# Interleaving two arrays: eight 32 KiB-row tiles in six buffers, or six 43 KiB-row tiles woven in place

## The chip, the cores and the metric

The kernel runs on one core of a Trainium2 chip. The metric is the device time of one execution in microseconds (us), as the median of several runs; lower is better. Five engines take part in different ways: SyncE (SP) and ScalarE (ACT) only issue DMAs here, VectorE (DVE) copies, TensorE and GpSimd do nothing for the result. All DMAs, from whichever queue, are carried by the core's 16 DMA engines, called rings here when one of them is meant.

## The reference

```python
batch, seq, dim = 32, 256, 1024          # x and y: float32, 33.6 MB each
result = np.zeros((batch, seq, dim * 2), dtype=np.float32)
result[..., 0::2] = x
result[..., 1::2] = y
```

Since `dim` is the last axis and contiguous, this is one interleaving of two flat arrays of 8,388,608 words: output word 2i is x[i], output word 2i+1 is y[i]. Nothing is calculated. 67.1 MB are read and 67.1 MB written.

## The kernel before

The flat arrays are cut into n = 8 tiles of 128 partitions with W = 8192 words (32 KiB) a partition. Each tile has 4 MiB of x, 4 MiB of y and 8 MiB of output. Six buffers of 32 KiB a partition are used: two for x (`xt`), two for y (`yt`) and two for woven output (`ot`). A tile's output does not fit into one `ot` buffer, so it is made in two halves h = 0 and 1, each of H = 4096 words of x and of y, and half h always uses `ot[h]`.

Three engines run one program each, tied together by semaphores:

- **SP, the loads.** L42 and L43 load the first x in two halves; these two DMAs are moved to the front of the program, ahead of the opening barrier. Then, for each tile, L50 loads x and L53 loads y. From the third tile on, L48 holds x until VectorE has done the last copy that reads this x buffer, and L52 holds y in the same way. The semaphore is `woven`, which VectorE raises after every copy.
- **VectorE, the weave.** For each half, L67 copies x into the even words of `ot[h]` and L70 copies y into the odd words. L60 and L69 wait for the loads. L64 waits until the earlier store of this `ot[h]` has landed. A landing counts 16 on a DMA's semaphore.
- **ACT, the stores.** L83 issues the store of a half when both its copies are done. The very first half is sent in two pieces, a quarter of its columns (8 KiB a row, L77) and the rest (24 KiB a row, L81).

The end (L87 to L93) waits for the last stores and clears the semaphores. The order of DMAs within a queue is the order of these loops; between the queues the hardware decides.

Of the kernel before, what the change touches and what calls it, by code (L numbers as in the profile page):

```python
# [3 lines left out]


def _interleave(nc, x, y, out):
    P = 128
    W = 8192
    H = W // 2  # L10

    total = 1
    for s in x.shape:
        total *= s
    n = total // (P * W)
    assert n * P * W == total

    def rows(ap, names, k):
        flat = ap.rearrange("b s d -> (b s d)")
        return flat[k * names : (k + 1) * names].rearrange("(p w) -> p w", p=P)  # L20

    fp32 = mybir.dt.float32
    xt = [nc.alloc_sbuf_tensor(f"xt{b}", [P, W], fp32).ap() for b in (0, 1)]
    yt = [nc.alloc_sbuf_tensor(f"yt{b}", [P, W], fp32).ap() for b in (0, 1)]
    ot = [nc.alloc_sbuf_tensor(f"ot{b}", [P, W], fp32).ap() for b in (0, 1)]

    xsem = [nc.alloc_semaphore(f"xsem{b}") for b in (0, 1)]
    hsem = nc.alloc_semaphore("hsem")
    qsem = nc.alloc_semaphore("qsem")
    ysem = [nc.alloc_semaphore(f"ysem{b}") for b in (0, 1)]  # L30
    woven = nc.alloc_semaphore("woven")
    osem = [nc.alloc_semaphore(f"osem{b}") for b in (0, 1)]


    cuts = [0, W // 4, W]
    parts = [slice(a, b) for a, b in zip(cuts, cuts[1:])]

    xs = [rows(x, P * W, k) for k in range(n)]
    ys = [rows(y, P * W, k) for k in range(n)]
    os_ = [rows(out, 2 * P * W, k) for k in range(n)]  # L40

    nc.sync.dma_start(out=xt[0][:, :H], in_=xs[0][:, :H]).then_inc(xsem[0], 16)  # L42
    nc.sync.dma_start(out=xt[0][:, H:], in_=xs[0][:, H:]).then_inc(hsem, 16)  # L43

    for k in range(n):
        b = k % 2
        if k >= 2:
            nc.sync.wait_ge(woven, 4 * (k - 2) + 3)  # L48
        if k:
            nc.sync.dma_start(out=xt[b], in_=xs[k]).then_inc(xsem[b], 16)  # L50
        if k >= 2:
            nc.sync.wait_ge(woven, 4 * (k - 2) + 4)  # L52
        nc.sync.dma_start(out=yt[b], in_=ys[k]).then_inc(ysem[b], 16)  # L53

    for k in range(n):
        b = k % 2
        for h in (0, 1):
            c = slice(h * H, (h + 1) * H)
            if h == 0:
                nc.vector.wait_ge(xsem[b], 16 * (k // 2 + 1))  # L60
            elif k == 0:
                nc.vector.wait_ge(hsem, 16)
            if k:
                nc.vector.wait_ge(osem[h], 16 * k)  # L64
            if (k, h) == (1, 0):
                nc.vector.wait_ge(qsem, 16)
            nc.vector.tensor_copy(out=ot[h][:, 0::2], in_=xt[b][:, c]).then_inc(woven, 1)  # L67
            if h == 0:
                nc.vector.wait_ge(ysem[b], 16 * (k // 2 + 1))  # L69
            nc.vector.tensor_copy(out=ot[h][:, 1::2], in_=yt[b][:, c]).then_inc(woven, 1)  # L70

    for k in range(n):
        for h in (0, 1):
            nc.scalar.wait_ge(woven, 4 * k + 2 * h + 2)
            if (k, h) == (0, 0):
                for c in parts[:-1]:
                    nc.scalar.dma_start(  # L77
                        out=os_[k][:, c], in_=ot[h][:, c]
                    ).then_inc(qsem, 16)
                c = parts[-1]  # L80
                nc.scalar.dma_start(out=os_[k][:, c], in_=ot[h][:, c]).then_inc(osem[h], 16)  # L81
                continue
            nc.scalar.dma_start(  # L83
                out=os_[k][:, h * W : (h + 1) * W], in_=ot[h]
            ).then_inc(osem[h], 16)

    nc.scalar.wait_ge(osem[0], 16 * n)  # L87
    used = sorted(s.num for s in [*xsem, hsem, qsem, *ysem, woven, osem[0]])
    assert used == list(range(used[0], used[-1] + 1)), used
    nc.scalar.sem_clear(range(used[0], used[-1] + 1))  # L90
    nc.sync.nop(nofuse=True).wait_op(osem[1], 16 * n, "sem-ge").then_inc(
        osem[1], -16 * n
    )  # L93


def kernel(tc, x, y, out):
    nc = tc.nc
    tc.close()
    tc.compile()

    _interleave(nc, x, y, out)

    blocks = nc.main_func.blocks
    for engine in (mybir.EngineType.SP, mybir.EngineType.SP):
        opening = blocks[0].instructions
        at, moved = next(
            (b, i)
            for b in blocks[1:]
            for i in b.instructions
            if i.engine == engine and i.opcode == "DMACopy"  # L110
        )
        assert not (moved.sync_info and moved.sync_info.on_wait)
        body = at.instructions
        body.remove(moved)
        gate = next(
            n
            for n, i in enumerate(opening)
            if i.engine == engine and i.opcode == "Drain"
        )
        opening.insert(gate, moved)  # L120
        at.instructions = body
        blocks[0].instructions = opening


# [1 line left out]
_INS = ['x', 'y']  # L126
_OUTS = [((32, 256, 2048), 'float32')]


# [23 lines left out]
```

## Time and profile before

| | |
|---|---|
| median of 3 runs | 314.21 us (314.18 to 314.25) |
| span of the profiled execution, first to last instruction | 312.9 us |
| time of the profiled execution | not listed apart; the median stands 1.35 us above the span of 312.86 |
| VectorE busy | 72.0 us, 32 copies of 2.29 us |
| DMA | 34 DMAs, 4896 packets, 134.22 MB, 429 GB/s over the span |
| HBM | 67.11 MB read, 67.11 MB written |
| store of 4 MiB, from issue to landing | 34.1 us median |
| load of y, 4 MiB, from issue to landing | 41.5 us median |

How to read it: a DMA's time from issue to landing holds the time that it stands in its queue behind others, so 34 us for 4 MiB says nothing of the speed of a transfer. The busy share of the DMA engines does, and the rate in GB/s beside it. In the timeline a row is an instruction (start, duration, engine, line, operation); for a DMA the duration is that of issuing it, not of the transfer. A bracket behind a row tells how long the engine had been idle and what released it.

### The profile page before, as it was taken

Reading aid. Unit: us, or ns where it says so; the run is one execution under the profiler, and the core shown is the slowest. Engines: PE = TensorE matmul, PEld = TensorE weight load, DVE = VectorE, ACT = ScalarE, POOL = GpSimd, SP = SyncE. Lnnn points to the kernel's source line nnn. Section 1 sums busy time; section 2 is a strip of 40 time slices with the busy share of each in tenths; the row PEclk is TensorE's granted clock in tenths of the full one; section 3 lists DMA queues with packets and bytes.
Section 4 is the critical chain, followed back from the end, with each engine's and each line's share of the span. In section 5 each row is a group of like instructions: output and inputs, shape, how many; then the busy total and the mean of one; then the engine's idle time right before and its main releaser. Section 6 shows DMA issues by size and latency. Waiting matters only on the chain.

```text
span 312.9 us, 114 instructions
## 1 busy us (share of the span) xinstructions
DVE 72.0 (23%) x32; POOL 0.2 (0%) x4
## 2 busy tenths in 40 slices
DVE  0216000501305023050220503205032050415410
POOL 0000000000000000000000000000000000000000
DMA  8999999999999999999999999999999999999998
GB/s 337 467 402 436 436 402 419 452 457 415 427 444 411 461 402 469 402 469 402 469 402 465 406 440 432 423 448 402 469 402 469 402 469 402 469 402 448 423 423 381
DMA packets 4896, 134.22 MB, mean 429 GB/s; under 512 B 544, under 2 KB 544, under 8 KB 544
## 3 DMA queue, kind: packets, MB, share of 16 engines
q1 hardware_dynamic: 2448, 67.11, 50.1%
q10 hardware_dynamic: 2448, 67.11, 49.7%
HBM read 67.11 MB, written 67.11 MB: 429 GB/s over the span
## 4 chain that ended last, share of the span: by engine, by line
DMA 82%; DVE 12%; issue 0%
DMA out_dram<-ot 76%; DMA yt<-in_y_dram 6%; DVE ot L70 6%; DVE ot L67 6%
## 5 line engine op out<-in xcount | busy, mean ns | idle before, releaser
L67 DVE COPY ot<-xt 128x4096 f32<-128x4096 f32 x16 | 36.7, 2295 | 213.8 <-DMA out_dram<-ot 206.5
L70 DVE COPY ot<-yt 128x4096 f32<-128x4096 f32 x16 | 36.6, 2288 | 12.3 <-DMA yt<-in_y_dram 12.3
L137 POOL MEMSET const-bfloat16-1.0<- 128x1 bf16 x1 | 0.1, 103 | 0.0
L137 POOL MEMSET const-uint8-127<- 128x1 uint8 x1 | 0.1, 102 | 0.0
L137 POOL MEMSET const-float32-0.0<- 128x1 f32 x1 | 0.1, 100 | 0.2 <-issue 0.2
L137 POOL MEMSET const-float32-1.0<- 128x1 f32 x1 | 0.1, 99 | 0.0
## 6 DMA issues: line engine op xcount, KB each, us to landing
out_dram<-ot ACTq DMA_DIRECT2D x15, 4096.0 KB, 34.1
yt<-in_y_dram SPq DMA_DIRECT2D x8, 4096.0 KB, 41.5
xt<-in_x_dram SPq DMA_DIRECT2D x7, 4096.0 KB, 24.3
xt<-in_x_dram SPq DMA_DIRECT2D x2, 2048.0 KB, 9.5
out_dram<-ot ACTq DMA_DIRECT2D x1, 3072.0 KB, 32.8
out_dram<-ot ACTq DMA_DIRECT2D x1, 1024.0 KB, 16.3
```

Of the source, the lines that this page charges most:

```text
L67: nc.vector.tensor_copy(out=ot[h][:, 0::2], in_=xt[b][:, c]).then_inc(woven, 1)
L70: nc.vector.tensor_copy(out=ot[h][:, 1::2], in_=yt[b][:, c]).then_inc(woven, 1)
L137: nc = _bacc.Bacc("TRN2", target_bir_lowering=False, num_devices=1)
```

## The change

The arrays are cut into six tiles, five with rows of 11008 words (43 KiB) and one with 10496 (41 KiB). Two regions `R[0]` and `R[1]` of 86 KiB a partition take the tiles in turn. A tile's x is loaded into the region's first half and its y into its second half, and the woven output is made in the same region: the low half of the output where x was, the high half where y was.

Weaving in place needs an order in which nothing is overwritten before it is read. VectorE first copies the upper half of x into a third buffer, `park`. It then spreads the lower half of x onto the even words of the low region in pieces that halve each time, from the top down (2752 words, 1376, and so on to 43); the last piece goes through the small buffer `last`, because its source and target overlap. When y is there, one copy puts the lower half of y on the odd words: the low half is complete and can be stored. Then the upper half of y is spread within its own region in the same way, and the parked x is laid on its even words. These are 21 copies a tile, 126 in all, and each waits for the one before it through the semaphore `step`.

The stores are one DMA for each half tile, 12 in all, and the loads 13 (the first x still in two pieces, of 4096 and 6912 words). From the third tile on SP holds the x load until the low half's store from that region has landed (`lsem`), and the y load until the high half's has (`hsem`). The two first loads are moved to the front as before, and the end waits for the last landings as before.

```diff
+TILES = [11008] * 5 + [10496]
+FIRST = 4096
...
-    xt = [nc.alloc_sbuf_tensor(f"xt{b}", [P, W], fp32).ap() for b in (0, 1)]
-    yt = [nc.alloc_sbuf_tensor(f"yt{b}", [P, W], fp32).ap() for b in (0, 1)]
-    ot = [nc.alloc_sbuf_tensor(f"ot{b}", [P, W], fp32).ap() for b in (0, 1)]
+    R = [nc.alloc_sbuf_tensor(f"R{b}", [P, 2 * N_MAX], fp32).ap() for b in (0, 1)]
+    park = nc.alloc_sbuf_tensor("park", [P, N_MAX // 2], fp32).ap()
+    last = nc.alloc_sbuf_tensor("last", [P, 64], fp32).ap()
...
+    def copy(to, of):
+        nonlocal count
+        if count:
+            nc.vector.wait_ge(step, count)
+        nc.vector.tensor_copy(out=to, in_=of).then_inc(step, 1)
+        count += 1
+
+    def halvings(m):
+        while m > 64:
+            assert m % 2 == 0
+            yield m // 2, m
+            m //= 2
+        yield 0, m
+
+    done = []
+    for k, N in enumerate(TILES):
+        b = k % 2
+        h = N // 2
+        X = R[b][:, :N]
+        Y = R[b][:, N : 2 * N]
+        low = R[b][:, :N]
+        high = R[b][:, N : 2 * N]
+
+        if k == 0:
+            nc.vector.wait_ge(fsem, 16)
+        nc.vector.wait_ge(xsem[b], 16 * (k // 2 + 1))
+        copy(park[:, :h], X[:, h:])
+        for i, j in halvings(h):
+            if i:
+                copy(low[:, 2 * i : 2 * j : 2], X[:, i:j])
+            else:
+                copy(last[:, :j], X[:, :j])
+                copy(low[:, 0 : 2 * j : 2], last[:, :j])
+        nc.vector.wait_ge(ysem[b], 16 * (k // 2 + 1))
+        copy(low[:, 1::2], Y[:, :h])
+        done.append([count])
+        for i, j in halvings(h):
+            i, j = h - j, h - i
+            if j < h:
+                copy(high[:, 2 * i + 1 : 2 * j : 2], Y[:, h + i : h + j])
+            else:
+                copy(last[:, : j - i], Y[:, h + i : h + j])
+                copy(high[:, 2 * i + 1 : 2 * j : 2], last[:, : j - i])
+        copy(high[:, 0::2], park[:, :h])
+        done[-1].append(count)
+
+    nc.sync.dma_start(out=R[0][:, :FIRST], in_=xs[0][:, :FIRST]).then_inc(fsem, 16)
+    nc.sync.dma_start(
+        out=R[0][:, FIRST : TILES[0]], in_=xs[0][:, FIRST:]
+    ).then_inc(xsem[0], 16)
+    for k, N in enumerate(TILES):
         b = k % 2
         if k >= 2:
-            nc.sync.wait_ge(woven, 4 * (k - 2) + 3)
+            nc.sync.wait_ge(lsem[b], 16 * (k // 2))
         if k:
-            nc.sync.dma_start(out=xt[b], in_=xs[k]).then_inc(xsem[b], 16)
+            nc.sync.dma_start(out=R[b][:, :N], in_=xs[k]).then_inc(xsem[b], 16)
         if k >= 2:
-            nc.sync.wait_ge(woven, 4 * (k - 2) + 4)
-        nc.sync.dma_start(out=yt[b], in_=ys[k]).then_inc(ysem[b], 16)
+            nc.sync.wait_ge(hsem[b], 16 * (k // 2))
+        nc.sync.dma_start(out=R[b][:, N : 2 * N], in_=ys[k]).then_inc(ysem[b], 16)
...
+    for k, N in enumerate(TILES):
         b = k % 2
...
+        for c, sem, ready in zip((0, N), (lsem[b], hsem[b]), done[k]):
+            nc.scalar.wait_ge(step, ready)
+            nc.scalar.dma_start(
+                out=os_[k][:, c : c + N], in_=R[b][:, c : c + N]
+            ).then_inc(sem, 16)
```

## The prediction

> **What bounds the kernel now.** I began with the page: the busy slices, the packet count and the two queues.
>
> ```profile
> DVE  0216000501305023050220503205032050415410
> ...
> DMA  8999999999999999999999999999999999999998
> ...
> DMA packets 4896, 134.22 MB, mean 429 GB/s; under 512 B 544, under 2 KB 544, under 8 KB 544
> ...
> q1 hardware_dynamic: 2448, 67.11, 50.1%
> q10 hardware_dynamic: 2448, 67.11, 49.7%
> ```
>
> The 16 DMA rings are busy in every slice; VectorE works a quarter of the time. q1 (SP's loads) and q10 (ACT's stores) split the span. 4896 packets are 34 DMAs of 128 rows (4352) and 16 semaphore packets for each (544): one row is one packet, whatever its length. Then the windows, for a stretch without start or end:
>
> ```profile
> 60.00:260.00 200.00, 47.04 (x21) 0.00 (x0) 1.00 1.00 433
> ```
>
> DMA share 1.00 at 433 GB/s. So the large waits are not losses, which is how I read this view:
>
> ```profile
> DVE ot L67 <- DMA out_dram<-ot: 206.5, 14, 29.0
> DVE ot L70 <- DMA yt<-in_y_dram: 12.3, 1, 12.3
> ```
>
> VectorE waits 206.5 us for output buffers while the rings work. Only two things can move the end: what a ring spends beside bytes, and moments in which it has no packet. The timeline shows the beginning and the end:
>
> ```profile
> 0.00 0.37 SPq L42 DMA_DIRECT2D xt<-in_x_dram  x1
> ...
> 21.91 2.29 DVE L70 COPY ot<-yt 128x4096 f32<-128x4096 f32 x1 [12.28 <-DMA yt<-in_y_dram]
> 24.12 2.29 DVE L67 COPY ot<-xt 128x4096 f32<-128x4096 f32 x1
> 24.24 0.38 ACTq L77 DMA_DIRECT2D out_dram<-ot  x1
> ...
> 293.53 2.29 DVE L67 COPY ot<-xt 128x4096 f32<-128x4096 f32 x1 [5.14 <-DMA out_dram<-ot]
> ```
>
> Stores land at 293.5 and, with the span's end, at 312.9: two stores in 19.3 us, 9.67 each, the full rate to the last row. Copies start 2.21 us apart for 4096 elements: 0.54 ns an element.
>
> The rest comes from the trace's packet records. On one ring, rows of 8, 16 and 32 KiB follow each other after 305.6, 606.6 and 1209.4 ns: bytes at 27.2 GB/s plus 4.2 ns a packet. A semaphore packet adds 6 ns. With both queues filled, a ring takes one row from each in turn. A ring carries 8.389 MB: 308.4 us, plus 272 rows x 4.2 ns = 1.14 and 34 x 6 ns = 0.20. The first row starts at 0.99 and the first rows are slow, 2.1 us in all. The sum is 311.85; the last packet ends at 312.48 and its count lands at 312.83. The missing 0.6 us stands in the load rows beside the first stores (27 to 43 us), which take up to 1.55 us in place of 1.21: 0.55 us a ring.
>
> The span is 312.86. The execution's own time is not listed apart; the runs' median, 314.21, is 1.35 above the span, and I keep these 1.35.
>
> **The change, part by part.** *Fewer, longer rows.* The DMAs fall from 34 to 25 (13 loads, 12 stores), the rows of a ring from 272 to 200. That is 72 x 4.2 ns = 0.30 us and 9 x 6 ns = 0.05 us, together **-0.36 us**, all on the path. A 43 KiB row at this law takes 1.623 us. No row over 32 KiB is in the trace; the law held over a factor of four, so I use it. The bounds: at best the whole overhead goes (-1.3); if each long row became two packets there would be 384 rows, 112 more than now, +0.5.
>
> *The first store.* Its 8 KiB piece (L77) goes; the first store now has 43 KiB rows. The 0.55 us of slow load rows lies just there: about 0.2 in the row before the first store row appears, 0.25 beside the 8 KiB rows, 0.07 at the second store. If it belongs to the beginning of writing it stays, if to short rows half of it goes. Bounds 0 and -0.55; I take **-0.15**, nearer to staying, because the largest part precedes the short rows.
>
> *When the first store starts.* x0 and y0 are 8 x 606.6 + 8 x 1020.7 + 8 x 1623 ns = 26.0 us, after the 2.1: y0's last row ends at 28.1 and not at 21.5. It costs nothing: x1 and y1 are queued (26 us of rows). Landing 0.38 after the last row, odd copy 5504 x 0.54 = 3.0, issue at 31.6. In the trace the first store row came 4.40 us after its issue (24.24 to 28.64), so 36.0 here; meanwhile four or five load rows run alone. From there rows alternate.
>
> *Loads that wait for stores.* L48 and L52 waited for the copy that had read a buffer; now the x of tile k+2 waits until the low store of tile k has landed, its y for the high one. Behind that wait on SP stands only the next y; VectorE would wait for both. Low 0 (8 pairs of 3.25 us) ends at 62, while x1 and y1 feed the rings until 72: some 9 us ahead, and as both queues then advance row for row this lead stays to tile 5. The Trainium skill's page "DMA: Bandwidth & Descriptors" (Anatomy of one DMA) speaks against this edit: most of a fixed 2 us lies between last byte and semaphore, worst with HBM as target. The trace has 0.35 us there, at a store (312.48 to 312.83); by the page 1.65 us more would come off a lead of 9, and the same off the tail's margin below.
>
> *The weave.* 126 copies for 32, 21 a tile, each waiting for the one before on `step`. Elements: four halves of 5504 a tile, 11.9 us. The 18 short ones add a fixed cost, not shown for DVE here; between 0.08 us (2.29 busy against 2.21 apart) and 0.3 us, three of the 0.10 us memsets. So 13 to 17 us a tile, up to 100 in all, under 52 us of DMA a tile. Parking x and spreading its half is done while y is still in transfer, a 26 us cover. Only the odd copy of the low half stands between y and a store: low 1 can be issued at 75.5 and is due when high 0 ends, at 88. If this cover were gone, every microsecond late would count once.
>
> *The tail*, where I expected a loss. When y5's last row ends, at E, the loads are over. After y0 there are 80 load rows a ring and as many store rows of tiles 0 to 4; they pair one for one, so the stores behind are as many as the load rows that ran alone before the first store: four or five, 6.5 to 8.1 us. E is near 278. Low 5 is issued at E + 0.38 + 2.85 + 0.05 = E + 3.3, so the rings stay fed if its first row comes within 3.2 us. The trace has two latencies: 0.99 us (first load, nothing else queued) and 4.40 us (first store, two whole loads queued on SP). In the tail SP is empty and ACT's rows go on, so I take the first: no gap, **0**, with 2 us or more to spare. High 5 is issued by E + 12, due at E + 19. The last two stores are 16 x 1.548 us.
>
> The Trainium skill has a rule that would change the tail: the same page (Queues, rings and completion order) lets a ring drain a packet of some 9 to 17 descriptors from one queue before it turns to the other. Nine are a whole DMA's share here; high 4 would then be untouched at E, 13 us of cover. The trace alternates single rows, so I keep 6.5.
>
> Sum: 314.21 - 0.36 - 0.15 = **313.7**.
>
> **The rivals.** *Faster, 313.2 to 313.5:* the slow load rows vanish with the 8 KiB piece: -0.36 - 0.55 = 313.3. For it: the second and third slow rows alternate with 8 KiB rows, and no later store shows any. Against it: the first slow row comes before any store row.
>
> *Slower, 314.9 to 315.4:* a gap in the tail. If low 5's first row comes 4.40 us after its issue, as the first store's did, the rings stand still for 3.3 + 4.4 - 6.5 = 1.2 us after high 4: 314.21 - 0.36 + 1.2 = 315.05 with the slow rows kept. It decides from 3.2 us of latency on; with one row less to cover, another 1.6 is lost. For it: 4.40 is the only latency beside other traffic that the trace shows unqueued. In the old tail low and high alternate through spare buffers and 4.45 us lay between issue and first row (288.43 to 292.87) without a gap, which excludes longer ones only. Against it: two loads stood ahead of the 4.40.
>
> *The change does not do what it says:* long rows are cut into two packets, 314.21 + 0.5 - 0.15 = 314.6. Also here: VectorE's longer program, fetched as 8 KiB packets. Those of the old kernel lie ahead of the span; one inside it would delay one ring by 0.3 us.
>
> **How the numbers follow.** 0.2% of 314.21 is 0.63 us, about what a measurement of this kernel can tell from no change: faster is under 313.58, slower over 314.84. Forecast (fed rings, most of the slow rows kept, 313.6 to 313.9) 0.40; slow rows gone 0.32; tail gap 0.16; cut rows or a fetch inside the span 0.07, mostly within; something unseen 0.05. Faster: 0.32 and a little of the forecast's lower edge, 0.36. Slower: 0.16 and most of the unseen, 0.20. Within: 0.44. The range reaches from 313.1 to 315.1, so that it holds both sides; the forecast's own is 313.5 to 313.9.
>
> **What would show it.** 25 x 144 = 3600 packets in place of 4896; a DMA share of 1.00 at 434 GB/s from 60 to 260 us; the first store issued near 31.6; low 5 issued about 3.3 us after y5 ends, near 282, and no thin slice there. Packets near 6540 would mean cut rows. A thin slice near 285 us would be the tail gap. Load rows still stretched beside the first store would put the time at 313.7 or above, none at 313.3. The forecast is wrong if the rate between 60 and 260 us is not 433 to 434 GB/s, if VectorE is still weaving low 5 when high 4 ends, or if SP's loads run dry before tile 5.

## The result

| | before | after |
|---|---|---|
| median (5 runs each, same chip) | 314.23 us (314.18 to 314.34) | 315.10 us (314.98 to 315.60) |
| ratio | | 1.003, 95% interval 1.002 to 1.0041 |
| span of the profiled execution | 312.9 us | 314.3 us (its own time 315.60, the slowest of the five) |
| DMA packets | 4896 | 3601 |
| VectorE copies | 32 | 126 |

The changed kernel is slower by 0.87 us, 0.3%. The forecast was 313.7 us in a range up to 315.1, so sign and size of the likeliest case were wrong. The page of the changed kernel, its busy slices and queues:

```profile
DVE 106.1 (34%) x126; POOL 0.2 (0%) x4
...
DVE  0093907204900900660350092071048026009300
...
DMA  9999999999999999999999999999999999999996
...
DMA packets 3601, 134.23 MB, mean 427 GB/s; under 512 B 400, under 2 KB 400, under 8 KB 400
...
q1 hardware_dynamic: 1872, 67.11, 49.9%
q10 hardware_dynamic: 1728, 67.11, 49.4%
q14 instruction: 1, 0.01, 0.0%
```

The packets fell as worked out: 25 DMAs give 25 x 144 = 3600. The last line is what the page of before does not have: one packet on queue 14, kind "instruction". Two stretches from the windows of both kernels; before first:

```profile
26.00:39.00 13.00, 2.61 (x2) 0.00 (x0) 1.00 1.06 441
```

and after:

```profile
26.00:39.00 13.00, 10.16 (x11) 0.00 (x0) 1.00 1.05 417
60.00:260.00 200.00, 66.33 (x75) 0.00 (x0) 1.00 1.00 433
```

Between 60 and 260 us nothing differs: 433 GB/s. The stretch in which stores begin is 24 GB/s thinner; this view books bytes to windows roughly (441 is more than the steady rate), so it says where to look and not how much. For the amounts I took the trace's packet records and joined them into rings: a packet belongs to the ring whose last packet ended where it starts. A row's excess is its duration over that of an undisturbed row of its size. The excess of load rows between 10 and 60 us, called the **stall** below, is 0.55 us a ring before (the mean of the 16 rings) and 1.17 after; after, it lies nearly all in one load row that ends where the ring's first store row starts. Each stall comes from one profiled execution. Taken from the starts of the rows in place of their durations it shifts by up to 0.04 us. The last packets end at 312.24 to 312.48 on the 16 rings before. After, 15 rings end at 312.26 to 312.79, and one at 313.91: the ring that carried the instruction packet.

The tail, where a gap was feared, in the timeline of the changed kernel:

```profile
282.99 6.98 DVE L52 COPY R<-R 128x5248 f32<-128x5248 f32 x8 [18.12 <-DMA R<-in_y_dram]
285.92 7.80 ACTq L112 DMA_DIRECT2D out_dram<-R  x2
```

Low 5 is issued at 285.92, and its rows follow high 4's on every ring without a pause, the first at 287.47. There is no gap.

### The profile page after: what moved, and what is told of

Same layout as the page of the kernel before. It is cut to its first block, busy times and chain, and to the rows that moved or that the text cites. A ratio compares the mean times of both kernels' runs of the same rounds, so it can differ in the third digit from the quotient of the medians.

```text
span 314.3 us, 205 instructions
## 1 busy us (share of the span) xinstructions
DVE 106.1 (34%) x126; POOL 0.2 (0%) x4
## 2 busy tenths in 40 slices
DMA packets 3601, 134.23 MB, mean 427 GB/s; under 512 B 400, under 2 KB 400, under 8 KB 400
## 4 chain that ended last, share of the span: by engine, by line
DMA 63%; another core or an unknown queue 22%; DVE 8%; SPq 0%; issue 0%; DVEq 0%
DMA R<-in_y_dram 25%; DMA out_dram<-R 23%; DMA R<-in_x_dram 15%; DVE R L52 6%; DVE park L52 1%; SPq L103 0%; DVE last L52 0%; SPq L106 0%; DVEq L51 0%
## 5 line engine op out<-in xcount | busy, mean ns | idle before, releaser
L52 DVE COPY R<-R 128x2752 f32<-128x2752 f32 (+11 forms) x90 | 65.5, 728 | 99.2 <-DMA R<-in_y_dram 96.3
L52 DVE COPY park<-R 128x5504 f32<-128x5504 f32 (+1 forms) x6 | 18.0, 3005 | 87.0 <-DMA R<-in_x_dram 87.0
L52 DVE COPY R<-park 128x5504 f32<-128x5504 f32 (+1 forms) x6 | 18.0, 3007 | 0.2
L52 DVE COPY R<-last 128x43 f32<-128x43 f32 (+1 forms) x12 | 2.2, 187 | 0.4
L52 DVE COPY last<-R 128x43 f32<-128x43 f32 (+1 forms) x12 | 2.2, 186 | 0.4
```

The lines of the kernel that those rows point to most:

```text
L52: nc.vector.tensor_copy(out=to, in_=of).then_inc(step, 1)
```

## The experiments

Each run stands beside runs of the kernel before on the same chip, whose medians were 314.19 to 314.27 us. Ratios are to these.

**First four: the two suspects, apart and together.** Run e1_short stops the halving earlier, so that VectorE has 78 copies:

```diff
-        while m > 64:
+        while m > 700:
-    last = nc.alloc_sbuf_tensor("last", [P, 64], fp32).ap()
+    last = nc.alloc_sbuf_tensor("last", [P, 704], fp32).ap()
```

> The changed kernel with the halving stopped at 688 words (a larger `last` buffer), so 13 copies a tile in place of 21, 78 in all; everything else as it is. Theory A (in the changed kernel one 8 KiB instruction-fetch packet at 91 us, asked for because VectorE's program is long, makes one of the 16 rings 1.2 us late, and that ring ends the kernel): no q14 packet in the span, all 16 final landings within 0.6 us, time 315.1 - 1.2 = 313.9 us (313.7 to 314.1). Rival B (one ring is late for another reason, the long rows or a busy port, and the fetch only stands nearby): a ring is still more than 1 us behind at the end, 315.0 to 315.2 us.

Measured: 315.51 us (315.21 to 316.22), 1.0044 [1.0032, 1.0056]. Neither theory's picture. The page still has the packet:

```profile
q14 instruction: 1, 0.01, 0.0%
```

It now lies at 165.3 us in place of 91.0. VectorE had begun 53 instructions of the trace by then in the changed kernel and 59 here, and the ring that carried it is again the last (313.54; the others 312.30 to 312.83). So the packet moved with the program and the late ring with the packet; the edit had not made the program short enough.

Run e2_piece gives the first store the old kernel's 8 KiB piece, e3_both has both edits:

```diff
+            if (k, c) == (0, 0):
+                nc.scalar.dma_start(
+                    out=os_[0][:, :PIECE], in_=R[0][:, :PIECE]
+                ).then_inc(psem, 16)
+                nc.scalar.dma_start(
+                    out=os_[0][:, PIECE:N], in_=R[0][:, PIECE:N]
+                ).then_inc(sem, 16)
+                continue
```

(`PIECE = 2048`; SP's first wait on `lsem` also waits on `psem`.)

> The changed kernel with the first store in two pieces as the old kernel had it: 8 KiB rows, then the rest of the low half. Theory C (each ring stands still when it turns to its first store row, longer for a longer row: 1.16 us for 43 KiB, 0.55 us in all with 8 KiB rows first): the stretch of load rows at the first store falls to about 0.55 us a ring, the time by 0.6 - 0.04 to 314.5 us (314.3 to 314.7). Rival D (the stall depends on the length of the load rows beside it, or on nothing that the piece changes): it stays at 1.1 to 1.2 us, time 315.1 us.

> Both edits together: 78 copies and the first store in two pieces. Theories A and C: 315.1 - 1.2 - 0.56 = 313.3 us (313.1 to 313.6), under the old kernel by 0.9; the DMA engines' packet overhead (-0.3 us) is then the only difference left beside the old kernel's start. B and D: 315.1. Only A true: 313.9. Only C true: 314.5.

Measured: 315.75 us (315.57 to 316.08), 1.005 [1.0038, 1.0062], and 315.24 us (314.85 to 316.21), 1.0037 [1.0025, 1.0049]. The stall fell, but only to 0.86 and 0.73 us: little at the 8 KiB rows, 0.5 to 0.8 in the load row before the first 35 KiB row. The times did not follow, for each still has a late ring (end 313.88 and 313.64, the others mostly 312.0 to 312.5). When one ring ends the kernel, what the other fifteen gain is not seen. Both expectations were missed.

Run e4_old_whole takes the 8 KiB piece from the old kernel:

```diff
-    cuts = [0, W // 4, W]
+    cuts = [0, W]
```

> The old kernel with its first store in one piece (32 KiB rows, no 8 KiB piece). Theory C: the stall at the first store grows from 0.55 toward what 32 KiB rows give, 0.8 to 1.0 us a ring, time 314.23 + 0.3 to 0.45 = 314.5 to 314.7 us. Rival D: it stays at 0.55 us (load rows are 32 KiB as before), time 314.2 us.

Measured: 314.47 us (314.37 to 314.63), 1.0008 [0.9999, 1.0017]; stall 0.82 us. With 32 KiB load rows on both sides of the comparison the stall is larger where the first store's rows are longer, and by theory C's amount. How far the same store varies is seen in e6_old_long below, which begins its stores as the kernel before does: 0.44 us against 0.55. The time's interval reaches down to 0.9999, so the time alone does not settle it; its 0.21 us is what 0.27 us of stall less 0.04 of packets should give.

**Then the fetch by itself.** Run e5_few shortens VectorE's program under the old kernel's by leaving out most of the weave (4 copies a tile):

```diff
-        for i, j in halvings(h):
...
+        copy(low[:, h : 2 * h : 2], X[:, h // 2 : h])
...
-        for i, j in halvings(h):
...
```

> The changed kernel with most of the weave left out: of each halving only the first piece of the low half is copied and none of the high half, so 4 copies a tile, 24 in all; loads, stores, waits and buffers as they are. The 78-copy kernel still had its fetch packet, only later (165 us in place of 91), both times after some 55 instructions of VectorE; the old kernel has 45 in all. Theory A (the fetch makes one ring late): now no q14 packet in the span, final landings within 0.6 us, the stall at the first store unchanged at 1.0 to 1.2 us a ring; time 314.23 - 0.36 + 0.6 = 314.45 us (314.2 to 314.6). Rival B (a ring is late for another reason): one ring still over 1 us behind, 315.1 to 315.5 us.

Measured: 314.74 us (314.31 to 315.11, 11 runs), 1.0014 [1.0005, 1.0022]. There is no instruction packet, and the page says so by its count:

```profile
DMA packets 3600, 134.22 MB, mean 428 GB/s; under 512 B 400, under 2 KB 400, under 8 KB 400
```

The stall is 1.07 us. Fourteen rings end at 312.33 to 312.62, but two at 313.22 and 313.27: after 60 us these two had lost 0.29 and 0.50 us in a few load rows. So the fetch is worth some 0.4 us of the median (315.10 or 315.16 less 314.74), and rival B has a part too: with these rows a ring can fall back without a fetch. Theory A's 314.2 to 314.6 us was missed.

Run e6_old_long puts the fetch into the old kernel:

```diff
             nc.vector.tensor_copy(out=ot[h][:, 1::2], in_=yt[b][:, c]).then_inc(woven, 1)
+            for p in range(4):
+                i = 8 * k + 4 * h + p
+                nc.vector.memset(pad[:, i : i + 1], 0.0)
```

(`pad` is a buffer of 64 columns that nothing else uses.)

> The old kernel with 64 one-column memsets added to VectorE's program, four behind each pair of copies; none is read by anything, and each takes some 0.1 us where VectorE is idle anyway. Theory A: an 8 KiB instruction fetch falls into the span after some 55 VectorE instructions, one ring ends 0.3 to 1.2 us late, time 314.26 + 0.3 to 1.2 = 314.6 to 315.4 us. Rival B: nothing changes on the rings, 314.2 to 314.3 us.

Measured: 314.79 us (314.71 to 315.13, 11 runs), 1.0019 [1.001, 1.0027]. On its page:

```profile
DMA packets 4898, 134.23 MB, mean 428 GB/s; under 512 B 545, under 2 KB 545, under 8 KB 545
...
q14 instruction: 2, 0.01, 0.0%
```

One of the two is a 32-byte packet at the very start; the other, of 8 KiB, lies at 177.9 us, when VectorE had begun 60 instructions. The ring that carried it ends at 313.03, the others at 312.11 to 312.40. On that ring the packet takes 0.31 us and the load row behind it 0.53 us more than its like: 0.84 us. All seven runs with a fetch show this pair, the second part between 0.53 and 0.54 us with rows of 32 and of 43 KiB. This is the cleanest run of the study: nothing but VectorE instructions in VectorE's idle time was added, and the DMA-bound kernel became 0.52 us slower. That is less than 0.84, because the ring that was hit would not have ended last by itself: it ends 0.63 us behind the next one.

**What the stall depends on.** Run e7_graded is e5_few with the first store in three pieces, run e8_old_cut moves the old kernel's cut:

```diff
+                cuts = [0, 3072, 6656, N]
+                for s, e, psm in zip(cuts, cuts[1:], (psem, tsem, sem)):
+                    nc.scalar.dma_start(
+                        out=os_[0][:, s:e], in_=R[0][:, s:e]
+                    ).then_inc(psm, 16)
```

(SP's first wait on `lsem` also waits on `psem` and `tsem`.)

```diff
-    cuts = [0, W // 4, W]
+    cuts = [0, 3328, W]
```

> The short-program kernel (24 copies, most of the weave left out) with the first store cut into three pieces of 12, 14 and 17 KiB a row. Theory E (a store row must be read almost whole before its writing begins, and a ring's reading is only some 0.44 us ahead when stores begin: 1.63 - 1.19 with 43 KiB rows, 1.21 - 0.76 with 32 KiB; the missing lead is paid once, at the first row that is longer than the lead): the stall at the first store falls to 0.2 to 0.3 us, but 0.5 to 1.0 us appears before the first 43 KiB store row (high 0); time within 0.3 of the run without pieces. Rival F (beginning to write to HBM costs once, by the length of the first rows): 0.2 to 0.3 us in all and nothing at high 0, time 0.8 us below the run without pieces, 313.6 us.

> The old kernel with the first store cut at 13 KiB (13 and 19 KiB a row) in place of 8 KiB (8 and 24). Theory E: 19 KiB rows take 0.72 us, so 0.72 - 0.44 = 0.3 us of stall in place of 0.55, time 314.26 - 0.25 = 314.0 us. Rival F: the first rows are longer than before, the stall grows to 0.6, time 314.3 us.

The runs of e7_graded lie between 314.14 and 321.02 us (12 runs; median 315.17, 1.0031 [1.001, 1.0051]), so F's 313.6 us did not come. Nothing here shows why this kernel varies so much. The profiled execution is the longest of the twelve, but the stall at the start can be read: 0.45 us a ring, most of it between 34 and 43 us, beside the 12 KiB rows, and about 0.1 at 57.8, beside the 14 KiB rows. Theory E looked for 0.5 to 1.0 us before high 0's first 43 KiB row. There is none, but the test was not the one that was meant: y1's last load rows had ended by 60.0 us and x2's first row came at 72.2, so no load row stood beside high 0's first rows at 67.3. F had 0.2 to 0.3 us in all; it was 0.45.

e8_old_cut: 314.32 us (314.14 to 314.41), 1.0002 [0.9993, 1.0011], stall 0.57. E's 0.3 is wrong, F's 0.6 about right, though 0.57 and the 0.55 of before are too close to tell a growth.

The same e7_graded execution has a gap in the tail, the rival that did not come about in the changed kernel. Windows of it:

```profile
278.00:287.00 9.00, 0.20 (x1) 0.00 (x0) 1.00 0.92 396
287.00:290.50 3.50, 3.47 (x2) 0.00 (x0) 1.00 0.12 50
290.50:312.00 21.50, 2.13 (x1) 0.00 (x0) 1.00 1.02 438
```

One ring had fallen back by several us; why is not shown, and no other kept execution has this, so it explains no difference between the kernels. y5 counts as landed only when the last ring has delivered its share, at 286.78; so low 5 was issued at 289.73, and the other rings had run out of rows at 287.0 to 287.4. The first row of low 5 came at 290.57, 0.84 us after the issue.

**Rows or order?** The last four. Run e9_rows32 keeps the order in place with 32 KiB rows and a short program (three copies a tile: the same `TILES`, and both halvings left out); e10_again is the changed kernel; e11_rows32_full is the changed kernel with 32 KiB rows and nothing left out; e12_old_three cuts the old first store in three, the second piece with a semaphore of its own:

```diff
-TILES = [11008] * 5 + [10496]
+TILES = [8192] * 8
```

```diff
-    cuts = [0, W // 4, W]
+    cuts = [0, 1024, 3072, W]
```

> The order of the changed kernel (two regions, in place, stores of half tiles, loads that wait for landings) with the old row length: eight tiles of 32 KiB rows. Most of the weave is left out: three copies a tile, 24 in all, so that VectorE's program is as short as the old one. Theory G (the rows' length makes the larger stall at the first store and lets late rings fall back further): stall 0.7 to 0.8 us a ring, as in the old kernel with its first store whole, final landings within 0.35 us, time 314.4 to 314.6 us, that kernel's 314.47. Rival H (the order in place does it, whatever the rows): stall over 1 us, rings 0.5 us or more apart at the end, 314.7 us or more, as the run with 43 KiB rows and 24 copies.

> The changed kernel itself, once more, beside the others of this call. Both theories: a fetch packet in the span near 91 us and one ring about 1 us behind, 315.0 to 315.6 us. It is the base against which the next two runs are read.

> The changed kernel with TILES = [8192] * 8, the whole weave in place with 32 KiB rows: the row length alone is undone. Theory G with A: the fetch (0.84 us on one ring, with no further loss, as in the old kernel with the long program), the 0.76 us stall, and the packets' 0.3 us back: 314.47 + 0.5 = 315.0 us, no better than the changed kernel. Rival H: also the ring's further losses, 315.4 us or more.

> The old kernel with its first store in three pieces of 4, 12-4 = 8 and 20 KiB a row. The cuts at 8 and at 13 KiB both gave 0.55 us of stall in all. Theory J (about half a microsecond is the price of turning from loads to mixed work, however short the first rows): 0.5 to 0.6 us again, 314.2 to 314.4 us. Rival K (the stall is the first row's time less what the reading is ahead): 4 KiB rows cost nothing, 20 KiB rows 0.3 us at most, 314.0 us, and this would be a version faster than both.

| run | median us (runs) | ratio to before, 95% | stall | ring ends |
|---|---|---|---|---|
| e9_rows32 | 314.47 (11) | 1.0008 [1.0, 1.0017] | 0.87 | 312.43 to 312.83 |
| e10_again | 315.16 (5) | 1.0034 [1.0021, 1.0047] | 1.19 | 312.24 to 312.83, fetch ring 313.38 |
| e11_rows32_full | 314.94 (11) | 1.0023 [1.0015, 1.0032] | 0.81 | all but one up to 312.82, fetch ring 313.30 |
| e12_old_three | 314.25 (11) | 1.0003 [0.9994, 1.0012] | 0.49 | 312.12 to 312.56 |

Theory G holds: with 32 KiB rows the order in place gives the time of the old kernel with its first store whole (314.47 both) and nearly its stall (0.87 and 0.82), and keeps its rings within 0.4 us. Two of its signs were a little small (0.8 and 0.35). Rival H falls.

Pairs of runs that differ mainly in one thing, as distances to the kernel before beside them, divide the loss (0.97 us in e10_again):

| what | us | from |
|---|---|---|
| the long program | 0.50, 0.47, 0.52 | e10_again less e5_few; e11_rows32_full less e9_rows32; e6_old_long |
| rows of 43 KiB in place of 32 | 0.22, 0.19 | e10_again less e11_rows32_full; e5_few less e9_rows32 |
| what stays with 32 KiB rows and a short program | 0.28 | e9_rows32; 0.21 of it also in e4_old_whole |

So about half of the loss is the program's length. The last row is the least certain, as both its intervals reach down to 1.

For e12_old_three theory J has the size right: in all the stall is again about half a microsecond, and there is no faster version on that way. But J's mechanism, a price of the turn itself, is not what the trace shows. Beside the 4 KiB rows the load rows lose only 0.02 us; 0.28 stands between 36 and 43 us, where the 8 KiB rows begin, and 0.19 between 49 and 60, where the 20 KiB rows begin. Rival K was right that 4 KiB rows cost nothing and wrong on the sum. In e2_piece and e3_both, too, the larger part stands where the rows become longer. No run here has a median below the old kernel's, and none points to a version that would.

## Why the prediction was wrong

| term | predicted | measured on the ring that ends last |
|---|---|---|
| fewer packets | -0.36 us | as worked out (below) |
| load rows at the first store | -0.15, bounds -0.55 and 0 | +0.62 (1.17 less 0.55 us, the mean of the rings) |
| instruction fetch | left out of the sum; 0.3 as a side case | +0.84, and +0.33 in later rows of the same ring |
| tail gap | 0 | 0 |

The sum of the right column is +1.43 us, and the last ring ends 313.91 - 312.48 = 1.43 us later than the last one before. That it fits so well is partly luck, for the two are not the same ring. The other 15 rings end 0.11 us later on average than the rings before (312.46 against 312.35), where the first two terms give 0.26. The profiled execution has 315.60 us; the median is lower, probably because the fetch falls on different rings: in e10_again on one that lost nothing more afterwards, and the last packet came at 313.38.

**Right:** the packet law. Rows of 43 KiB follow each other after 1.623 us, 44032 bytes at 27.2 GB/s and 4.2 ns; they were not cut. The rate between 60 and 260 us came as worked out, and so did the loads that wait for landings: from x2 to y5 each was issued 9 to 10.5 us before SP's rows ahead of it ended, so the lead was never used up. The first store was issued at 31.56 (31.6 forecast).

**Right in effect, wrong in the sum:** the weave. "Four halves of 5504 a tile" should be five: x's upper half is copied twice, into `park` and out of it. VectorE was busy for 106.1 us and not "up to 100". The transfers cover it, so it cost nothing.

**Right in effect, one step wrong:** the tail. The working let a load's count land 0.38 us after its last row. That held for y0, when no store was queued yet. With both queues filled the count, a packet of 4 bytes, waits for its turn behind a whole row of the other queue. On one ring y5's last row ends at 279.35, a store row follows, the 4-byte packet starts at 280.96 and the count lands at 281.34: 2.0 us, of which 1.62 are the store row. The same row is most of what made low 1 late, issued at 78.28 and not at 75.5, still 7 us before high 0's last rows ended:

```profile
75.22 7.25 DVE L52 COPY R<-R 128x5504 f32<-128x5504 f32 x8 [18.12 <-DMA R<-in_y_dram]
78.28 8.06 ACTq L112 DMA_DIRECT2D out_dram<-R  x2
```

In the tail this row and the spread of the rings (y5's last rows end between 279.35 and 281.00, and the late ring alone decides when VectorE may start) made low 5 later than E + 3.3: it was issued 4.9 us after y5's last row on the latest ring. It cost nothing because the cover was longer as well, 8.1 us on the first ring (279.35 to 287.47) and not 6.5. That the two nearly cancel is luck. Low 5 was issued 1.55 us before its first row, so with a latency of 1 us some 0.6 us were to spare where "2 us or more" had been said. The choice of the 0.99 us latency over the 4.40 was right: the rows came 1.55 us after the issue without a pause. The prediction also held a 1.65 us delay of the count against the edit, from the Trainium skill's page "DMA: Bandwidth & Descriptors" (Anatomy of one DMA). That section is on DMAs issued by GpSimd, and those here are issued by SP and ACT. A delay of that size did come off the tail's margin, but as the turn behind one row; from the end of the 4-byte packet to the count it was 0.37 us.

**Wrong, first step: the bound of the first store's term.** I took its 0.55 us as a price that could only stay or fall, and set the end of the range at 0. The rows that begin the stores became longer by the same edit, and in the runs the term grows with them: 0.44 to 0.57 us with first rows of 4, 8 and 13 KiB in the old kernel, 0.81 to 0.87 with 32, about 1.1 to 1.2 with 43. Nothing in the trace of before excluded a rise; an upper bound from a whole first row (1.2 us there) would have been open to it. The old kernel's small first piece has a use: without it, in e4_old_whole, the stall rises by 0.27 us. The prediction also gave 0.07 us to the second store and then said, for the rival, that no later store shows any; e12_old_three has most of the term at its later pieces.

**Wrong, second step: the fetch.** "VectorE's longer program" stood among the side cases with 7 in 100 for it and another together, mostly within 0.2%. Two things were at hand. The trace of before showed all 8 KiB fetches ahead of the span with 45 VectorE instructions, and the change made them 144. From how many instructions on one falls inside the trace could not tell, but with three times as many it deserved a term of its own. And its price was taken as the packet alone (0.3 us), without the 0.53 us that the next load row loses. What it is worth in time is 0.47 to 0.52 us, about half of the loss. The Trainium skill's page "Runtime: NRT & Kernel Launch" (Instruction fetch mechanics) says that a sequencer fetches ahead through a DMA queue of its own, in blocks of 16 KiB, and that the cost is mostly hidden. The trace agrees on the queue (q14). The packet in the span has 8 KiB, and its cost is not hidden here: a ring that is never idle pays 0.84 us.

**Then why slower at all?** The fewer packets earn 0.36 us and the first store's longer rows lose about 0.6. In e5_few, without a fetch, the 14 rings in step end only about 0.1 us later than before (312.44 against 312.35 on average). The rest of its 0.47 us comes from the two rings that fall back, and in the changed kernel the fetch adds another 0.5.

**Open:** why a ring that is late loses more when rows are 43 KiB long. The losses lie in single load rows, in e5_few in those that directly follow the semaphore packet that ends a store (for instance 0.24 us at 113.8 us), on the changed kernel's fetch ring in rows that follow a store row (190.9 and 258.7 us). They are mostly on rings half a microsecond or more behind, but not on every such ring (e10_again's fetch ring lost nothing more); with 32 KiB rows the late rings of e6_old_long and e11_rows32_full showed none. What makes the stall grow with the store's rows is not settled either: the lead model failed in e8_old_cut and, as rival K, in the sum of e12_old_three.

## What to carry to other kernels

In a kernel bound by DMA everything that uses a ring is on the path, the instructions of an idle engine too: count each engine's instructions before and after a change, and look at the instruction queue in the list of queues. A DMA counts as landed, and the kernel as ended, with its slowest ring, so a delay on one of 16 rings counts from where it makes this ring the last, while a gain on 15 is not seen. Where a change makes transfers longer, bound a cost beside them by the new length, not by what the cost was. And when a wait is for the count of a DMA, look for what stands in the other queue ahead of that count.

## What the runs showed of the hardware

- In every run whose VectorE program was long (96 to 174 traced instructions), an 8 KiB instruction packet appeared on one ring when VectorE had begun 53 to 60 of them; in those with 42 to 46 in all there was none. It costs that ring 0.31 + 0.53 us, and the kernel 0.47 (e11_rows32_full less e9_rows32) and 0.52 us (e6_old_long).
- Where stores join the loads, between 24 and 60 us, the load rows of a ring lose 0.4 to 1.2 us in all, more with longer store rows, and in e12_old_three at the steps to longer rows; afterwards rows of both queues alternate at 433 GB/s.
- The count of a DMA is a packet of its own on each ring. With both queues filled it waited for one row of the other queue (1.62 us with 43 KiB rows), and landed 0.37 us after its own end.
- The first row of a store came 0.84 us after its issue on empty rings (one execution, e7_graded) and 5.35 us after it with two whole loads queued (31.56 to 36.91 in the changed kernel, the stall of 1.2 included).
